# A 31-tap depthwise convolution: from taps on two engines to column-tiled products over shifted copies

## The chip, the cores and the metric

One core of one Trainium2 chip. The metric is the device time of one execution of the whole program in microseconds (us): 3539.51, the median of 3 runs.

## The reference, cut to what matters

Two blocks of two layers each. Block 1 has 768 tokens in its first layer (512 and a context of 256) and carries 512 on from the second. A layer's mixer has three branches; the third is a gated unit followed by a depthwise convolution along the tokens, with 31 taps for each of 256 channels. The other branches: `chunk_gmlp` (gated token mixing) and differential attention.

```python
def dwconv(x, w, b):
    k = w.shape[0]
    y = lax.conv_general_dilated(
        x, w[:, None, :].astype(x.dtype), window_strides=(1,), padding=[(k // 2, k // 2)],
        dimension_numbers=("NWC", "WIO", "NWC"), feature_group_count=x.shape[-1])
    return y + b

def conformer_conv(pc, P):
    a, g = jnp.split(pc, 2, axis=-1)
    y = dwconv(a * jax.nn.sigmoid(g), P["conv_w"], P["conv_b"])
    return jax.nn.silu(layer_norm(y, P["ln_c_g"], P["ln_c_b"]))

def chunk_gmlp(pa, P):
    z = jax.nn.gelu(pa)
    u, v = jnp.split(z, 2, axis=-1)
    v = layer_norm(v, P["ln_v_g"], P["ln_v_b"])
    b, n, _ = v.shape
    vb = v.reshape(b, n // CHUNK, CHUNK, A_HEADS, A_HEAD_DIM)
    gate = jnp.einsum("hpq,bnqhd->bnphd", P["w_s"], vb) + P["b_s"].T[:, :, None]
    return u * gate.reshape(b, n, A_WIDTH)

    # of a block, for each layer:
    pa, q, k, v, pc = project(h, P, rope)
```

The two segments (512 tokens and 256) are convolved each for itself.

## The kernel before

**Products.** A product of precision fp32 is made of three matmuls (L639) over pairs of a rounded part `h` and a rest `l`. Weights stream from HBM in pieces `wr` (two buffers, L274, issued by the sync queue, SP); ScalarE rounds a piece to `wh` (L286), VectorE subtracts to get `wl` (L287); there are three buffers of each. `need` asks for a piece and has the next ones loaded and split (two splits and four loads ahead).

**A layer of block 1** (`b1_layer`). The products of the convolution branch come first (`c`), their results go through the gate (`glu`, L984 on ScalarE, L985 on VectorE; in layer 0 the first half of the channels also through L1059 and L1060) into `cy`: channels on partitions, two tiles of 128 channels, a segment of 512 tokens and in layer 0 one of 256, with 15 zeros at each end. Then follow the products `at` (gated token mixing, six banks of 128 tokens in layer 0, four in layer 1; eight pieces of the contraction), `kt` (keys, six banks in both layers), `qt` (queries) and `vt` (values). A pool of six PSUM banks serves them in turn.

**What lies between `at` and `kt`.** ScalarE takes the gelu of each bank into `z` (L1143). VectorE normalises half of it: statistics (L1145, L1146), the inverse root (L405 to L414), three steps for each `z` (L1153 to L1155). Then TensorE multiplies by the gate's weights (`gt`, L1158: four matmuls of 64 columns), VectorE applies the gate (L1161), TensorE transposes (`yaT`, L1164). The order of TensorE's instructions has these among the matmuls of `kt`.

**Side work.** Each `need` calls `aside`: one or two steps of the modulation vectors (`gv`, L357: a step is four column-tiled fp32 matmuls with 32 columns of weights and 512 moving columns; the trace shows two records for each matmul), whose inputs `g` are loaded by SP (L316, two buffers), and four taps of the convolution.

**Taps.** `ca` gathers the result. The first channel tile is VectorE's: a tap is one instruction for each segment (L1114). The second is GpSimd's: a multiplication into a part of `Q` (L1117), an addition (L1118). Tap 0 is ScalarE's (L1112). `conv(31)` after `kt` asks for what is left.

**What sets the order.** A list scheduler puts each engine's instructions, SP's transfers among them, in one order; each engine runs them in it, and an instruction waits at its place for what it needs.

Of the kernel before, what the change touches and what calls it, by code (L numbers as in the profile page):

```python
# [20 lines left out]
P = 128  # L21
# [107 lines left out]
def _conv(w):  # L129
    """[taps, C] -> [128, C/128 * taps]"""  # L130
# [15 lines left out]
def make_cols():  # L146
    """Per-channel vectors, channels on partitions."""
# [35 lines left out]
def make_mix_cols(l):  # L183
    """What the mixer of a layer of block 1 needs on chip besides its weights."""
    return _layout([
        ("cw", 62, lambda I: _conv(I["conv_w"][l])),
# [12 lines left out]

def bias_table(rpb):  # L200
    """[8, 15, 31] -> [8, 128 (row of the pair, query column), 14 * 64 (row offset, key column)], masked
    outside the window."""
# [16 lines left out]
# ---------------------------------------------------------------- the program  # L219
class Kern:  # L220
    def __init__(self, ctx, tc, ap):
# [20 lines left out]
        # weight stream  # L242
# [7 lines left out]
        # the weights of an output product wait until the attention before it is under way  # L250
# [3 lines left out]
        self.kept = {}  # pools of weights that stay for both parts of the tokens  # L254
# [14 lines left out]
    # -- weights: loaded and split ahead of their use  # L269
# [42 lines left out]
    # -- conditioning vectors  # L312
# [73 lines left out]
    def gemv_until(self, layer, n=1):  # L386
        """At most the vectors of the layers before this one."""
# [9 lines left out]
    # -- small pieces  # L397
# [665 lines left out]
    def b1_layer(self, l, norm):  # L1063
# [11 lines left out]
        with ExitStack() as kvc:  # L1075
# [5 lines left out]
            with ExitStack() as c:  # L1081
# [38 lines left out]
                for t in range(31):  # L1120
                    tap(1, t)
# [694 lines left out]
```

## Time and profile before

| | us |
|---|---|
| median of 3 runs (3536.82 to 3546.21) | 3539.51 |
| span of the profiled execution | 3542.8 |
| TensorE busy in it | 3361.6 |
| VectorE busy | 2431.3 |
| ScalarE busy | 1384.4 |
| GpSimd busy | 353.8 |

The page has no time for the profiled execution other than its span, which lies within the range of the runs. Busy time is a sum over the whole span; the windows and the timeline show single stages. A row of a timeline gives the start, the duration, the engine, the line and the operation, what is written and read, and the idle time before it with what ended it. Matmuls are pipelined: the distance of their starts, not their duration, tells what each costs. `b1l0` is layer 0 of block 1, `b1l1` layer 1.

### The profile page before, as it was taken

How to read it: one execution, taken by the hardware profiler on the slowest of the kernel's cores; microseconds unless marked ns; L12 is line 12 of the kernel's file. 1: busy time of each engine (PE TensorE's matmuls, PEld its weight loads, DVE VectorE, ACT ScalarE, POOL GpSimd, SP SyncE). 2: the span in 40 equal slices, each digit the busy share in tenths (PEclk: the TensorE clock that was granted, in tenths of full speed). 3: DMA queues.
4: the chain of work that ended last, by engine and by line, in shares of the span. 5: the costliest groups of instructions: out<-in, count | busy, mean ns of one | idle time of the engine just before them, and what ended most of it. 6: DMA issues, size and time to landing. Idle time of an engine off the chain costs nothing.

```text
span 3542.8 us, 49269 instructions
## 1 busy us (share of the span) xinstructions
PE 3361.6 (95%) x19440; PEld 2803.6 (79%) x19440; DVE 2431.3 (69%) x4171; ACT 1384.4 (39%) x2548; POOL 353.8 (10%) x310
## 2 busy tenths in 40 slices
PE   8589899999996889999999999999999999999998
PEld 5366788888885679877887778888888878898887
DVE  6967857565559786888653887667564777765445
ACT  4115742222233265222423775312222556653233
POOL 1930000000007210000101111000000100010001
PEclk9899999999998899999999999999999999999999
DMA  6233214333321113555422013344332220032332
GB/s 235 84 101 95 87 48 143 109 122 107 110 90 52 55 43 119 171 180 179 139 82 66 24 35 102 96 125 129 120 104 66 84 61 19 13 114 89 96 95 72
DMA packets 106775, 341.72 MB, mean 96 GB/s; under 512 B 12528, under 2 KB 15600, under 8 KB 106544
## 3 DMA queue, kind: packets, MB, share of 16 engines
q1 hardware_dynamic: 106544, 338.57, 30.9%
q8 instruction: 153, 2.51, 0.3%
q14 instruction: 78, 0.64, 0.1%
HBM read 318.27 MB, written 9.44 MB: 93 GB/s over the span
## 4 chain that ended last, share of the span: by engine, by line
PE 83%; DVE 8%; ACT 2%; issue 1%; DMA 1%; ACTq 0%; POOLq 0%; POOL 0%; DVEq 0%
PE b1l0o L639 2%; PE b2l0o L639 1%; PE b2l1o L639 1%; PE b2l0y L639 1%; PE b1l0y L639 1%; PE b1l1o L639 1%; DVE b1l1ca L1114 1%; PE b1l0qt L639 1%; PE b2l0qat L639 1%; PE b2l1qp L639 1%; PE b2l0vbt L639 1%; PE b1l0vt L639 1%; DVE wl L287 1%; PE gv L367 1%; PE b1l0kt L639 1%
## 5 line engine op out<-in xcount | busy, mean ns | idle before, releaser
L286 ACT CAST wh<-wr 128x1024 fp32r<-128x1024 f32 (+2 forms) x368 | 355.6, 967 | 877.2 <-issue 86.3
L287 DVE TENSOR_TENSOR wl<-wr,wh 128x1024 fp32r<-128x1024 f32 (+2 forms) x368 | 422.1, 1148 | 354.5 <-ACT wh L286 351.6
L341 DVE SCALAR_TENSOR_TENSOR ga<-g,cv,ga 128x1024 f32<-128x1024 f32 x252 | 310.0, 1279 | 4.5 <-DMA g<-in_wmod_dram 4.1
L1114 DVE SCALAR_TENSOR_TENSOR b1l0ca<-b1l0cy,b1l0half,b1l0ca 128x512 f32<-128x512 f32 (+1 forms) x60 | 74.8, 1298 | 0.0
L1118 POOL TENSOR_TENSOR b1l0ca<-b1l0Q,b1l0ca 128x512 f32<-128x512 f32 (+1 forms) x60 | 74.1, 1255 | 0.2
L1117 POOL TENSOR_TENSOR b1l0Q<-b1l0cy,b1l0half 128x512 f32<-128x512 f32 (+1 forms) x60 | 62.4, 1059 | 73.6 <-DVE b1l0cy L985 73.6
L357 PE MATMUL gv<-g,sil 128*32 128x512 f32 x128 | 32.2, 658 | 29.0 <-DMA g<-in_wmod_dram 28.9
L1087 POOL MEMSET b1l1cy<- 128x30 f32 x1 | 0.1, 127 | 584.2 <-PE b1l0y L639 584.2
L493 POOL TENSOR_TENSOR b2l0nas<-b2l0rx,b2l0rx 128x512 f32<-128x512 f32 (+1 forms) x2 | 3.4, 1686 | 535.6 <-DVE b2l0rx L813 535.6
L1403 POOL TENSOR_SCALAR b1l1rx<-b1l1rx 128x768 f32<-128x768 f32 x8 | 17.1, 2135 | 382.0 <-ACT b2l0t0c L581 371.7
L1118 POOL TENSOR_TENSOR b1l1ca<-b1l1Q,b1l1ca 128x512 f32<-128x512 f32 x30 | 47.5, 1584 | 1.2
L1114 DVE SCALAR_TENSOR_TENSOR b1l1ca<-b1l1cy,b1l1half,b1l1ca 128x512 f32<-128x512 f32 x30 | 44.2, 1472 | 1.1 <-issue 0.6
L1117 POOL TENSOR_TENSOR b1l1Q<-b1l1cy,b1l1half 128x512 f32<-128x512 f32 x30 | 42.0, 1418 | 29.1 <-issue 29.1
L1158 PE MATMUL b1l1gt<-b1l1z,b1l1mc 128*128 128x64 f32 x32 | 5.9, 348 | 40.3 <-DVE b1l1z L1155 36.6
L1158 PEld LDWEIGHTS b1l1gt<-b1l1z,b1l1mc 128*128 128x128 f32 x32 | 5.7, 260 | 41.4 <-DVE b1l1z L1155 37.0
L493 POOL TENSOR_TENSOR b2l1a2s<-b2l1rx,b2l1rx 128x256 f32<-128x256 f32 x2 | 2.3, 1161 | 347.4 <-DVE b2l1rx L1378 347.4
L357 PEld LDWEIGHTS gv<-g,sil 128*32 128x32 f32 x128 | 4.4, 112 | 40.9 <-DMA g<-in_wmod_dram 34.3
L493 POOL TENSOR_TENSOR b2l1nas<-b2l1rx,b2l1rx 128x256 f32<-128x256 f32 x2 | 1.5, 742 | 344.3 <-DVE b2l1rx L813 344.3
L850 POOL TENSOR_TENSOR b2l0q<-b2l0QA,b2l0q 64x768 fp32r<-64x768 f32 x6 | 11.3, 1884 | 184.9 <-DVE b2l0VB L682 151.1
L370 ACT COPY gs<-gv 128x512 f32<-128x512 f32 x24 | 14.1, 587 | 36.5 <-PE gv L357 28.7
L858 POOL TENSOR_TENSOR b1l0K<-b1l0KT,b1l0K 64x768 fp32r<-64x768 f32 x6 | 10.9, 1817 | 148.7 <-ACT b1l0K L857 148.5
L343 DVE TENSOR_SCALAR ga<-g,cv 128x1024 f32<-128x1024 f32 x36 | 25.5, 747 | 0.0
(11665 smaller groups left out, 12138.7 us busy)
## 6 DMA issues: line engine op xcount, KB each, us to landing
wr<-in_wts_dram SPq DMA_DIRECT2D x288, 512.0 KB, 3.6
g<-in_wmod_dram SPq DMA_DIRECT2D x176, 512.0 KB, 4.0
wr<-in_wts_dram SPq DMA_DIRECT2D x64, 384.0 KB, 3.1
wr<-in_wts_dram SPq DMA_DIRECT2D x64, 320.0 KB, 2.9
b1l0KT<-in_wmod_dram SPq DMA_DIRECT2D x6, 512.0 KB, 7.0
b1l0Q<-in_wmod_dram SPq DMA_DIRECT2D x6, 512.0 KB, 8.6
inx<-in_x_dram SPq DMA_DIRECT2D x8, 384.0 KB, 8.9
b1l0K<-b1l0K SPq DMA_DIRECT2D x16, 192.0 KB, 2.8
```

What stands on the lines that cost most here:

```text
L286: self.nc.scalar.copy(hi, raw)
L287: self.nc.vector.tensor_tensor(out=lo, in0=raw, in1=hi.bitcast(F32), op=SUB)
L341: nc.vector.scalar_tensor_tensor(out=self.gacc[c], in0=g, scalar=v, in1=self.gacc[c], op0=MUL, op1=ADD)
L343: nc.vector.tensor_scalar(out=self.gacc[c], in0=g, scalar1=v, scalar2=None, op0=MUL)
L357: nc.tensor.matmul(self.gacc[32 * e:32 * e + 32, :], self.sil[:, 2 * k + j, :], g[:, h * 512:h * 512 + 512], start=k == 0, stop=k == 3, ti ...
L367: nc.tensor.matmul(self.gacc[32 * e:32 * e + 32, :], self.ones[:, 0:32], acc[c][:, h * 512:h * 512 + 512], tile_position=(0, 32 * e))
L370: nc.scalar.copy(s, self.gacc)
L639: self.last_mm = self.nc.tensor.matmul(o, s, m[:, sl], start=start and j == 0, stop=stop and j == 2)
L1114: nc.vector.scalar_tensor_tensor(out=dst, in0=src, scalar=s, in1=dst, op0=MUL, op1=ADD)
L1117: nc.gpsimd.tensor_tensor(out=m, in0=src, in1=s.to_broadcast([P, w]), op=MUL)
L1118: nc.gpsimd.tensor_tensor(out=dst, in0=m, in1=dst, op=ADD)
L1403: nc.gpsimd.tensor_scalar(out=X[d], in0=X[d], scalar1=ALPHA, scalar2=None, op0=MUL)
```

## The change

The convolution becomes products. Four shifted copies of the gated input lie under one another on the partitions: group `4 i + k` of `XS` holds, in its partitions 32 j to 32 j + 31, channels 32 k to 32 k + 31 of channel tile `i`, shifted by `j` tokens. A matmul whose stationary operand `cw` (128 x 32: for each of the four shifts a diagonal of 32 tap weights) meets such a group does four taps for 32 channels; eight of them, each four tokens further on, do all 31 (the 32nd weight is zero). The four `k` write to the four quarters of the columns (`tile_position=(0, 32 * k)`) of one bank. ScalarE then halves the result, adds the bias and writes `ca`.

The copies are transfers from SBUF to SBUF on SP: 64 in layer 0 (32 partitions of 540 values, or of 284 for the segment of 256 tokens), 32 in layer 1. `XS` lies in one tile `U` with `KT` and `Q`, which come to be written after it is read. `cw` comes as an input of its own (`convw`, 1 MB for each layer) by a transfer of its own. `Q` no longer lends its place to GpSimd's products, nor to the last two `z`. The products stand between those of `kt` and of `qt`. The taps, and their place in `aside`, are gone. The rest of the diff takes comments out.

```diff
+C_TAPS = 31
-        ("cw", 62, lambda I: _conv(I["conv_w"][l])),
...
+def conv_blocks(w):
+    out = np.zeros((4, 32, 2, 8, 4, 32), np.float32)
+    c = np.arange(32)
+    for t in range(C_TAPS):
+        out[t % 4, c, :, t // 4, :, c] = w[t].reshape(2, 4, 32).transpose(2, 0, 1)
+    return out.reshape(P, 2048)
...
-            KT = kv.tile([P, 4, T], F32, name=b + "KT")
-            Q = kv.tile([P, nq, 512], F32, name=b + "Q")
+            span = sum(w + 28 for _, w in segs)
+            U = kv.tile([P, max(8 * span, 4 * T + nq * 512)], F32, name=b + "U")
+            XS = U[:, :8 * span].rearrange("p (g w) -> p g w", w=span)
+            KT = U[:, :4 * T].rearrange("p (h t) -> p h t", t=T)
+            Q = U[:, 4 * T:4 * T + nq * 512].rearrange("p (t d) -> p t d", d=512)
             Kr = kv.tile([P, 6, 512], F32, tag="KV", name=b + "Kr")
-            cy = [kv.tile([P, 2, w + 30], F32, name=b + f"cy{r}") for r, (_, w) in enumerate(segs)]
+            cy = [kv.tile([P, 2, w + 31], F32, name=b + f"cy{r}") for r, (_, w) in enumerate(segs)]
...
-                half = self.sm.tile([P, 62], F32, tag="half", name=b + "half", bufs=1)
-                nc.vector.tensor_scalar(out=half, in0=self.mcol("cw"), scalar1=0.5, scalar2=None, op0=MUL)
-                ca = [self.xp.tile([P, T], F32, tag="x", name=f"{b}ca{i}") for i in range(2)]
+                cw = c.enter_context(tc.tile_pool(name=b + "cw", bufs=1, reuse_waits="tile")).tile([P, 2, 8, 4, 32], F32, name=b + "cw")
+                nc.sync.dma_start(out=cw, in_=self.ap["convw"][l].rearrange("p (i g k c) -> p i g k c", i=2, g=8, k=4))
+                offs = [sum(w + 28 for _, w in segs[:r]) for r in range(len(segs))]
+                for i in range(2):
+                    for r, (_, w) in enumerate(segs):
+                        for k in range(4):
+                            for j in range(4):
+                                nc.sync.dma_start(out=XS[32 * j:32 * j + 32, 4 * i + k, offs[r]:offs[r] + w + 28],
+                                                  in_=cy[r][32 * k:32 * k + 32, i, j:j + w + 28])
+                ca = []
+
+                def conv():
+                    for i in range(2):
+                        ca.append(self.xp.tile([P, T], F32, tag="x", name=f"{b}ca{i}"))
+                        for r, (x0, w) in enumerate(segs):
+                            ps = pp.tile([P, w], F32, tag="mm", name=f"{b}cv{i}{r}")
+                            for g in range(8):
+                                for k in range(4):
+                                    nc.tensor.matmul(ps[32 * k:32 * k + 32, :], cw[:, i, g, k], XS[:, 4 * i + k, offs[r] + 4 * g:offs[r] + 4 * g + w],
+                                                     start=g == 0, stop=g == 7, tile_position=(0, 32 * k))
+                            nc.scalar.activation(out=ca[i][:, x0:x0 + w], in_=ps, func=AF.Identity, scale=0.5, bias=self.mcol("cb", i, 1))
+
                 tmp = c.enter_context(tc.tile_pool(name=b + "pt", bufs=2, reuse_waits="tile"))
-                def tap(i, t):
...
-                for t in range(31):
-                    tap(1, t)
...
-                    conv(4)
...
-                    z = (self.xp.tile([P, T], F32, tag="x", name=f"{b}z{i}") if i < 4 else
-                         Q[:, i])
+                    z = self.xp.tile([P, T], F32, tag="x", name=f"{b}z{i}")
...
-                conv(31)
+                conv()
                 ps = self.tproj(pp, b + "q", H, no, 512, b + "q")
```

SP in layer 0, around the first weights of `kt`. A number behind a name tells buffers apart. Before, `wr_570` is the last piece of `at`'s weights, `wr_812` the first of `kt`'s:

```order
L274 DMA wr_570<-in_wts_dram 128x1024
L274 DMA wr_812<-in_wts_dram 128x1024
L316 DMA g_831<-in_wmod_dram 128x1024
L316 DMA g_833<-in_wmod_dram 128x1024
L316 DMA g_889<-in_wmod_dram 128x1024
L274 DMA wr_883<-in_wts_dram 128x1024
```

The same place after; `wr_569` is the last piece of `at`'s weights, `wr_754` the first of `kt`'s:

```order
L1124 DMA b1l0U<-b1l0cy_137 32x540 x4
L284 DMA wr_569<-in_wts_dram 128x1024
L1124 DMA b1l0U<-b1l0cy_137 32x540 x14
L1124 DMA b1l0U<-b1l0cy_138 32x284 x16
L1124 DMA b1l0U<-b1l0cy_137 32x540 x14
L1124 DMA b1l0U<-b1l0cy_138 32x284 x16
L284 DMA wr_754<-in_wts_dram 128x1024
L326 DMA g_765<-in_wmod_dram 128x1024
```

The two pieces of weights stood next to one another; now 60 copies stand between them. In layer 1 two copies come ahead of the third piece of `at`'s weights, ten ahead of the fourth, and twenty between that and the first of `kt`'s.

VectorE in layer 0, before, where it splits the second piece of `kt`'s weights (`wr_883`) and comes to the statistics of `z`:

```order
L1114 SCALAR_TENSOR_TENSOR b1l0ca_675<-b1l0cy_139,b1l0half,b1l0ca_675 128x256
L382 TENSOR_TENSOR mod_2_1008<-gt_1003,cols 128x8
L287 TENSOR_TENSOR wl_996<-wr_883,wh_995 128x1024
...
L1114 SCALAR_TENSOR_TENSOR b1l0ca_675<-b1l0cy_138,b1l0half,b1l0ca_675 128x512
L1145 BN_STATS b1l0bst_1062<-b1l0z_1060 128x6
```

After, the end of the steps on `z` and the split of the first piece of `kt`'s weights (`wr_754`):

```order
L1166 TENSOR_TENSOR b1l0z_980<-b1l0z_980,b1l0mc 128x256
L1166 TENSOR_TENSOR b1l0z_985<-b1l0z_985,b1l0mc 128x256
...
L1166 TENSOR_TENSOR b1l0z_995<-b1l0z_995,b1l0mc 128x256
L297 TENSOR_TENSOR wl_864<-wr_754,wh_863 128x1024
```

Two pieces of `kt`'s weights were split ahead of the statistics; now the first is split behind all steps on `z`.

TensorE after, layer 0, from the end of `kt` to the first matmuls of `qt`:

```order
L649 MATMUL b1l0kt_1140<-wh_1200,inHl_121 128x512
L649 MATMUL b1l0kt_1140<-wh_1200,inHh_120 128x512
L649 MATMUL b1l0kt_1140<-wl_1201,inHh_120 128x512
L1136 MATMUL b1l0cv_1461<-b1l0U,b1l0cw 32x512 x32
L1136 MATMUL b1l0cv_1495<-b1l0U,b1l0cw 32x256 x32
L1136 MATMUL b1l0cv_1530<-b1l0U,b1l0cw 32x512 x32
L1136 MATMUL b1l0cv_1564<-b1l0U,b1l0cw 32x256 x32
L367 MATMUL gv_1610<-g_1260,sil 32x512 x2
L367 MATMUL gv_1610<-g_1262,sil 32x512 x2
L649 MATMUL b1l0qt_1598<-wh_1250,inHl_107 128x512
L649 MATMUL b1l0qt_1598<-wh_1250,inHh_106 128x512
```

The convolution's 128 matmuls stand in one piece, with no other product among them.

## Rows read from the trace of the kernel before

**Rows 1.** The page, parts 1 and 4: busy us (share); shares of the chain

```profile
PE 3361.6 (95%) x19440; PEld 2803.6 (79%) x19440; DVE 2431.3 (69%) x4171; ACT 1384.4 (39%) x2548; POOL 353.8 (10%) x310
...
PE 83%; DVE 8%; ACT 2%; issue 1%; DMA 1%; ACTq 0%; POOLq 0%; POOL 0%; DVEq 0%
```

**Rows 2.** Windows: length; busy (instructions) of each engine; PEclk, DMA share, GB/s

```profile
170.00:180.00 10.00, 0.00 (x0) 0.00 (x0) 9.96 (x12) 0.00 (x0) 10.00 (x11) 0.51 0.00 1
228.00:320.00 92.00, 91.47 (x420) 63.26 (x412) 65.80 (x188) 27.28 (x41) 0.00 (x0) 1.00 0.42 135
1107.00:1195.00 88.00, 45.96 (x187) 36.15 (x186) 71.94 (x81) 9.42 (x17) 70.07 (x50) 0.73 0.12 36
```

**Rows 3.** The page, part 5: busy us, mean ns | idle before

```profile
L1114 DVE SCALAR_TENSOR_TENSOR b1l0ca<-b1l0cy,b1l0half,b1l0ca 128x512 f32<-128x512 f32 (+1 forms) x60 | 74.8, 1298 | 0.0
...
L357 PEld LDWEIGHTS gv<-g,sil 128*32 128x32 f32 x128 | 4.4, 112 | 40.9 <-DMA g<-in_wmod_dram 34.3
```

**Rows 4.** Timeline of TensorE in the two layers: start, duration, what, [idle before]

```profile
71.91 0.39 PE L639 MATMUL b1l0at<-wh,inHl 128*128 128x512 f32 x1
...
146.33 1.92 PE L357 MATMUL gv<-g,sil 128*32 128x512 f32 x4 [20.35 <-DMA g<-in_wmod_dram]
...
184.14 1.94 PE L1158 MATMUL b1l0gt<-b1l0z,b1l0mc 128*128 128x64 f32 x8 [16.65 <-issue]
...
227.64 1.06 PE L357 MATMUL gv<-g,sil 128*32 128x512 f32 x8
...
1084.71 0.39 PE L639 MATMUL b1l1at<-wh,b1l0Hl 128*128 128x512 f32 x1
...
1162.61 1.97 PE L1158 MATMUL b1l1gt<-b1l1z,b1l1mc 128*128 128x64 f32 x8 [36.57 <-DVE b1l1z L1155]
...
1194.81 0.40 PE L639 MATMUL b1l1qt<-wh,b1l0Hl 128*128 128x512 f32 x1
```

**Rows 5.** Chain of waits, 60 to 330 us: start, us, engine, what, records

```profile
208.21 0.84 PE b1l0gt L1158 x8
...
220.01 7.70 PE b1l0kt L639 x33
...
227.71 0.99 PE gv L357 x8
```

**Rows 6.** Timeline of TensorE, two modulation steps back to back

```profile
34.47 1.48 PE L357 MATMUL gv<-b1l0KT,sil 128*32 128x512 f32 x10
...
35.79 0.60 PE L357 MATMUL gv<-b1l0Q,sil 128*32 128x512 f32 x2
```

**Rows 7.** All transfers of line 1675, its own view: count, min/median/max ns

```profile
L1675 SPq DMA_DIRECT2D b2l1kh<-b2l1kh x3: 573/584/591, 2861.0 to 2865.4; - x3
...
DMA to landing us min/median/max: 2.1/2.6/3.8
```

**Rows 8.** Timeline of SP, copies of 64 partitions

```profile
322.73 8.02 SPq L860 DMA_DIRECT2D b1l0K<-b1l0K  x8
```

**Rows 9.** The page, part 6: issues, KB each, us to landing

```profile
wr<-in_wts_dram SPq DMA_DIRECT2D x288, 512.0 KB, 3.6
```

**Rows 10.** Timeline of VectorE: gated input of layer 0, of layer 1

```profile
74.75 2.97 DVE L1060 SCALAR_TENSOR_TENSOR b1l0cy<-b1l0cy,b1l0cbs,b1l0KT 128x512 f32<-128x512 f32 x2
...
1087.72 0.68 DVE L985 SCALAR_TENSOR_TENSOR b1l1cy<-b1l1cy,b1l1c10L 128x512 f32<-128x512 f32 x1
```

**Rows 11.** Timeline of ScalarE after `at` of layer 0

```profile
119.38 1.30 ACT L1143 ACTIVATE b1l0Q<-b1l0at 128x512 f32<-128x512 f32 x2
...
120.58 1.04 ACT L286 CAST wh<-wr 128x1024 fp32r<-128x1024 f32 x1
```

**Rows 12.** VectorE by line, 228 to 300 us: busy us, mean ns

```profile
L287 DVE TENSOR_TENSOR wl<-wr,wh 128x1024 fp32r<-128x1024 f32 x6 | 7.3, 1224 | 1.3 <-ACT wh L286 1.3
...
L947 DVE TENSOR_TENSOR b1l0kns<-b1l0Kr,b1l0kS 128x256 f32<-128x256 f32 x8 | 3.0, 419 | 0.0
...
L413 DVE SCALAR_TENSOR_TENSOR b1l0knr2q<-b1l0knr2q,b1l0knr2h 128x16 f32<-128x16 f32 x3 | 0.5, 177 | 0.1
```

More of the change, by code (lines that the diff above doesn't have):

```diff
@@ L1087, in b1_layer @@
                     nc.gpsimd.memset(cy[r][:, :, 0:15], 0.0)
-                    nc.gpsimd.memset(cy[r][:, :, w + 15:w + 30], 0.0)
+                    nc.gpsimd.memset(cy[r][:, :, w + 15:w + 31], 0.0)
                 if last:
@@ L1102, in b1_layer @@
                     nc.sync.dma_start(out=self.mcols, in_=self.ap["mcols"][l])
-                half = self.sm.tile([P, 62], F32, tag="half", name=b + "half", bufs=1)
-                nc.vector.tensor_scalar(out=half, in0=self.mcol("cw"), scalar1=0.5, scalar2=None, op0=MUL)
-                ca = [self.xp.tile([P, T], F32, tag="x", name=f"{b}ca{i}") for i in range(2)]
-                tmp = c.enter_context(tc.tile_pool(name=b + "pt", bufs=2, reuse_waits="tile"))
-                def tap(i, t):
-                    for r, (x0, w) in enumerate(segs):
-                        src, dst, s = cy[r][:, i, t:t + w], ca[i][:, x0:x0 + w], half[:, 31 * i + t:31 * i + t + 1]
-                        if t == 0:
-                            nc.scalar.activation(out=dst, in_=src, func=AF.Identity, scale=s, bias=self.mcol("cb", i, 1))
-                        elif i == 0:
-                            nc.vector.scalar_tensor_tensor(out=dst, in0=src, scalar=s, in1=dst, op0=MUL, op1=ADD)
-                        else:
-                            m = Q[:, t % 2 * 2 + r, :w]
-                            nc.gpsimd.tensor_tensor(out=m, in0=src, in1=s.to_broadcast([P, w]), op=MUL)
-                            nc.gpsimd.tensor_tensor(out=dst, in0=m, in1=dst, op=ADD)
@@ L1120, in b1_layer @@
-                for t in range(31):
-                    tap(1, t)
-                taps = [(0, t) for t in range(31)]
-                def conv(n):
-                    for a in taps[:n]:
-                        tap(*a)
-                    del taps[:n]
+                cw = c.enter_context(tc.tile_pool(name=b + "cw", bufs=1, reuse_waits="tile")).tile([P, 2, 8, 4, 32], F32, name=b + "cw")
+                nc.sync.dma_start(out=cw, in_=self.ap["convw"][l].rearrange("p (i g k c) -> p i g k c", i=2, g=8, k=4))
@@ L1799, in host_arrays @@
         "mcols": np.stack([np.concatenate([f(I) for _, _, f in make_mix_cols(l)[0].values()], axis=1) for l in range(2)]),
+        "convw": np.stack([conv_blocks(I["conv_w"][l]) for l in range(2)]),
         "bias": c(bias_table(I["l0_rpb_2"])),
```

## The prediction

> **What bounds the kernel now.** I read the page first. TensorE is busy for 95% of the span, and the chain of work that ended last is TensorE for 83% and VectorE for 8% [rows 1]. So time is won only where TensorE stands still, and the windows say where that is. From 228 to 320 us it is busy for 91.47 of 92.00 us: work saved elsewhere doesn't help there, and what is won ahead of it is kept. In the key product of layer 1 (1107 to 1195) it is busy for 45.96 of 88 us, while VectorE is busy for 71.94 and GpSimd for 70.07. In the 10 us from 170 both of these are busy throughout, TensorE does nothing, and its granted clock is 0.51, its 1.2 GHz level [rows 2]. What they do there is the taps: 60 on VectorE in layer 0 at 1298 ns [rows 3], on GpSimd two instructions for each tap.
>
> The timeline of TensorE shows what these holes wait for [rows 4]. Layer 0, from the first `at` at 71.91 to the modulation step at 227.64, takes 155.7 us. It has a hole of 20.35 us that ends with a transfer of `g`, and one of 16.65 us before the gate's first product. Neither is a slow transfer: on VectorE the split of the weights and the normalisation of `z` stand among taps, the sync queue waits for the split, and `g` waits in that queue. In layer 1, from 1084.71 to 1194.81 (110.1 us), the hole is 36.57 us, ended by VectorE's last step on `z`.
>
> **Part 1: the taps go.** VectorE and GpSimd lose all of them. What TensorE then has between the same two points, at full clock, is: 144 matmuls of `at` and 144 of `kt` at 7.70/33 = 0.233 us, 67.2 us; eight modulation steps at 0.99, 7.9; six gate products at 0.84, 5.0 [rows 5]; some 2.3 for transposes, an estimate. Layer 0: 82.4 us. In layer 1, 96 and 144 matmuls give 56.0, four gates 3.4, transposes 0.9: 60.3 us.
>
> **Part 2: the convolution becomes TensorE's work.** Layer 0 gets 64 matmuls of 512 columns and 64 of 256, in groups of four, one for each quarter of the columns; layer 1 gets 64 of 512. They stand between `kt` and `qt`, where nothing covers them: they count in full. The nearest thing in the trace is the modulation step, four column tiles of 32 with fp32 operands and 512 columns. Two such steps, 16 records in four passes, begin at 34.47 and their last records at 35.79: (35.79 - 34.47)/3 = 0.44 a pass, two passes to a group, 0.88 us [rows 6]. So layer 0 pays 16 x 0.88 + 16 x 0.44 = 21.1 us and layer 1 14.1 us. A step by itself took 0.99 [rows 5]; by that price the two layers would pay 4 us more, the upper bound. Evacuation is four reads by ScalarE in layer 0 and two in layer 1 (six banks are there, `qt` needs those of `kt` first): nothing.
>
> Each weight load of such a step took 0.112 us [rows 3], and passes 0.44 apart leave no room for two of them to each matmul [rows 6]. The Trainium skill (TensorE: Matmul & The Clock Gate, Part 3: Packing small matmuls) says that a weight load overlaps running matmuls only where the row group differs, and here all four share it. By that rule the loads would be exposed; the trace doesn't agree, with passes 0.44 apart. What it would cost is a rival below.
>
> **Part 3: the copies.** 64 transfers of 32 partitions in layer 0 and 32 in layer 1 enter the sync queue. They are ordered behind the gated input, and ahead of the first weights of `kt`, of the `g` behind these, and of all that follows. No transfer of before is just that. The nearest is the copy of 32 partitions from SBUF to SBUF, at a median 584 ns of issue and 2.6 us to land [rows 7]. I take 0.6 us each, since with that spacing five are under way at a time. The bound above is the row of eight copies of 64 partitions, 8.02/8 = 1.0 us [rows 8]; below, half of 0.6 if issue is shorter for half the bytes.
>
> Layer 0: the first part of the gated input is ready at 74.75 + 2.97/2 = 76.2 [rows 10]. Then 64 x 0.6 = 38.4, and 0.6 for a load of `at` between them: `kt`'s weights are issued at 115.2, land 3.6 us later [rows 9], are rounded in 1.04 [rows 11] and subtracted in 1.22 [rows 12]: ready at 121.0. `at` ends at 71.91 + 33.6 + 1.0 for a modulation step + 0.4 for the tail of the product before it = 106.9. A **new wait of 14.1 us**. VectorE alone would give nearly the same: the order puts that subtract behind the whole `z` chain, which is 106.9 + 0.65 for a gelu + 0.6 for statistics (estimate) + 11 x 0.177 for the root + 18 x 0.42 + 1.22 = 118.9 [rows 11, 12]. So a faster queue wins 2 us at most.
>
> Layer 1: the second half of the copies follows the gated input at 1087.72 + 0.68 = 1088.4 [rows 10]; 20 x 0.6 later the weights are issued, at 1100.4, and could be ready at 1106.3. There the subtract stands behind the root and three steps of `z`: `at` ends at 1107.1, and 0.65 + 0.6 + 1.9 + 3 x 0.42 + 1.22 = 5.7 gives 1112.8. A wait of 5.7 us.
>
> I add 6 us in layer 0 and 4 in layer 1 for what else can be late: matmuls at half clock after the new wait, the splits of `at`'s last weights, and `g`. This is a choice, between 0 and twice as much.
>
> **Sum.** Layer 0: 82.4 + 21.1 + 14.1 + 6 = 123.6 against 155.7, 32.1 won. Layer 1: 60.3 + 14.1 + 5.7 + 4 = 84.1 against 110.1, 26.0 won. Together 58.1. The span of the profile, 3542.8, lies within the runs and 3.3 above their median, so I take the gain from the median: 3539.5 - 58.1 = **3481 us**. The matrix loads with the copies (1 MB more for each layer) are issued tens of us ahead and are costed at nothing; if the first held up `at`, it would be by the landing of one load, some 4 us.
>
> **Rivals.**
>
> *Less late than I allow.* The 10 us of allowances are not needed and the queue is quick: 12 us less, 3469. For it: after 228 the same engines keep TensorE at 99%. Against it: every hole of before left matmuls at half clock behind it.
>
> *The queue takes 1.0 us for a copy.* Then layer 0 loses 64 x 0.4 = 25.6, layer 1 (1088.4 + 20 + 5.9 = 1114.3 against 1112.8) 1.5: 3508. For it, the row of 64 partitions [rows 8]; against it, that those move twice the partitions.
>
> *Weight loads exposed.* Eight loads of 0.112 for each of 48 groups, 43 us: 3524. Against it speak the 0.44 us between passes [rows 3, 6].
>
> *Slower: the queue becomes the bound.* The copies come at p us each, and all weights of `kt` stand behind them. The gain is 58.1 - 64 (p - 0.6) - 20 (p - 0.93), nothing at p = 1.37. If a copy had to land before the next one, at the least landing of 2.1 us [rows 7], it would be 58.1 - 96 - 23.4 = -61: 3601. For it: no stretch of before has 64 copies in a row. Against it: these rows start copies 0.6 apart with landings of 2.6. The Trainium skill (DMA: Bandwidth & Descriptors, Rules for kernel authors) says that under 64 KB a transfer is mostly overhead, with about 2 us of fixed cost; the copies have 69 and 36 KB, and taken in turn they would cost what this rival says. The rows agree with the 2 us as a landing time, not as a spacing.
>
> *Slower too: column tiles of the convolution don't run side by side.* Three times the price is added, 3 x (21.1 + 14.1) = 106: 3587. Only [rows 6] speaks against it, but plainly.
>
> **How the numbers follow.** Forecast 3481, by itself 3468 to 3497 with the allowances and bounds above: 63%. Less late 10%; queue at 1.0 us 17%; loads exposed 4%; queue as bound 4%; tiles in turn 2%. About 0.3% (10.6 us) is what a measurement of this kernel can tell from no change, so the edge is at 3529: faster 0.90, same 0.04 (the upper ends of the second and third rivals), slower 0.06. The range of 8 in 10 leaves out the last three rivals and the upper part of the second: 3461 to 3515.
>
> **What would show it.** In the profile after: no taps and no holes of 20, 17 and 37 us; one wait before `kt` of about 14 us (layer 0) and 6 (layer 1), ended by VectorE's split of the weights; the convolution's groups 0.88 us apart, 21 and 14 us in all; copies 0.6 apart. Wrong: copies 1 us or more apart, a wait before `qt` for copies, passes of 0.87, or waits for `g` in the later part of `kt`.

## The result, and the profile after

The changed kernel takes **3493.56 us** (median of 4 runs, 3491.70 to 3496.89), the kernel before 3540.56 in the same session (4 runs, 3536.82 to 3546.21): a ratio of 0.9862 with a 95% interval of 0.9848 to 0.9876, 47 us or 1.4% faster. The forecast was 3481, its range 3461 to 3515. The profiled executions differ by more than the medians do, 3542.8 against 3490.3 us, since the one of before lies 2 us above its median and the one of after 3 us below.

Parts 1 and 4 of the page of after, which answer to [rows 1]. TensorE has 384 records more (192 matmuls, two records each) and 27 us more of work, GpSimd 222 us less; TensorE's share of the chain that ended last is 91% instead of 83%.

```profile
PE 3388.5 (97%) x19824; PEld 2814.2 (81%) x19824; DVE 2263.5 (65%) x4079; ACT 1383.5 (40%) x2548; POOL 131.5 (4%) x130
...
PE 91%; DVE 5%; ACT 2%; DMA 1%; issue 1%; SPq 0%; ACTq 0%; POOLq 0%; POOL 0%; DVEq 0%
```

Windows of both layers, from the first `at` to the end of the modulation step behind `kt`, or to the first `qt` (length; busy of PE, PEld, DVE, ACT, POOL; PEclk, DMA share, GB/s), of before:

```profile
71.91:228.64 156.73, 104.16 (x431) 67.02 (x430) 137.65 (x169) 25.46 (x41) 134.40 (x120) 0.83 0.26 85
1084.71:1194.81 110.10, 68.06 (x282) 53.85 (x281) 92.13 (x96) 20.05 (x31) 88.38 (x60) 0.78 0.14 43
```

and of after:

```profile
74.65:207.47 132.82, 118.77 (x688) 72.25 (x686) 55.55 (x167) 28.41 (x45) 0.00 (x0) 0.95 0.41 129
1063.21:1146.14 82.93, 78.10 (x409) 54.83 (x408) 38.57 (x105) 21.60 (x34) 0.00 (x0) 0.96 0.29 83
```

Layer 0 is 23.9 us shorter, layer 1 27.2. Of the other 1.4 us of the difference of the two spans, `at` begins 2.7 us later (74.65 against 71.91) and the rest behind layer 1 takes 3.8 us less. No run ties either to the change: three of the kernels below have the order of after up to that point, on every engine, and begin `at` at 71.97, 72.45 and 74.85. For the 3.8 us no run shows a cause.

The timeline of TensorE, which answers to [rows 4] (start, duration, what, idle before): one wait ahead of layer 0's `kt`, two short ones in layer 1, and the convolutions where the step behind `kt` and the first `qt` wait for them.

```profile
123.88 0.79 PE L649 MATMUL b1l0kt<-wh,inHl 128*128 128x512 f32 x1 [14.04 <-ACT wh L296]
...
185.83 20.85 PE L1136 MATMUL b1l0cv<-b1l0U,b1l0cw 128*32 128x512 f32 x256
206.50 1.04 PE L367 MATMUL gv<-g,sil 128*32 128x512 f32 x8
...
1087.39 0.51 PE L649 MATMUL b1l1kt<-wh,b1l0Hl 128*128 128x512 f32 x1 [1.62 <-ACT wh L296]
...
1091.57 0.80 PE L649 MATMUL b1l1kt<-wl,b1l0Hh 128*128 128x512 f32 x1 [3.21 <-DVE wl L297]
...
1132.27 13.94 PE L1136 MATMUL b1l1cv<-b1l1U,b1l1cw 128*32 128x512 f32 x128
1146.14 0.51 PE L649 MATMUL b1l1qt<-wh,b1l0Hl 128*128 128x512 f32 x1
```

The timelines of the sync queue, ScalarE and VectorE around that wait. 60 copies follow each other in 39.23 us, 0.654 us each; the first weights of `kt` are issued behind them, at 119.01; ScalarE waits 12.25 us for that transfer and rounds it, and `kt` begins. VectorE has been done with `z` since 119.5 and waits too.

```profile
76.25 2.75 SPq L1124 DMA_DIRECT2D b1l0U<-b1l0cy  x4
...
79.68 39.23 SPq L1124 DMA_DIRECT2D b1l0U<-b1l0cy  x60
119.01 0.53 SPq L284 DMA_DIRECT2D wr<-in_wts_dram  x1
```

```profile
122.79 1.04 ACT L296 CAST wh<-wr 128x1024 fp32r<-128x1024 f32 x1 [12.25 <-DMA wr<-in_wts_dram]
```

```profile
118.77 0.75 DVE L1166 TENSOR_TENSOR b1l0z<-b1l0z,b1l0mc 128x256 f32<-128x256 f32 x2
123.86 1.23 DVE L297 TENSOR_TENSOR wl<-wr,wh 128x1024 fp32r<-128x1024 f32 x1 [4.35 <-ACT wh L296]
```

### The profile page after: what moved, and what is told of

Same layout as the page of the kernel before. It is cut to its first block, busy times and chain, and to the rows that moved or that the text cites. A ratio compares the mean times of both kernels' runs of the same rounds, so it can differ in the third digit from the quotient of the medians.

```text
span 3490.3 us, 49902 instructions
## 1 busy us (share of the span) xinstructions
PE 3388.5 (97%) x19824; PEld 2814.2 (81%) x19824; DVE 2263.5 (65%) x4079; ACT 1383.5 (40%) x2548; POOL 131.5 (4%) x130
## 4 chain that ended last, share of the span: by engine, by line
PE 91%; DVE 5%; ACT 2%; DMA 1%; issue 1%; SPq 0%; ACTq 0%; POOLq 0%; POOL 0%; DVEq 0%
PE b1l0o L649 2%; PE b2l0o L649 1%; PE b2l1o L649 1%; PE b1l1o L649 1%; PE b2l0y L649 1%; PE b1l0y L649 1%; PE b1l0kt L649 1%; PE b1l1kt L649 1%; PE gv L367 1%; PE b1l0qt L649 1%; PE b1l0at L649 1%; PE b1l1vt L649 1%; PE b1l0vt L649 1%; PE b2l0qat L649 1%; PE b2l1qp L649 1%; PE b2l0vbt L649 1%
## 5 line engine op out<-in xcount | busy, mean ns | idle before, releaser
L649 PE MATMUL b1l0kt<-wh,inHl 128*128 128x512 f32 x48 | 20.0, 416 | 14.0 <-ACT wh L296 14.0
L380 ACT COPY gs<-gv 128x512 f32<-128x512 f32 x24 | 14.1, 586 | 39.4 <-PE gv L367 32.4
L353 DVE TENSOR_SCALAR ga<-g,cv 128x1024 f32<-128x1024 f32 x36 | 25.5, 746 | 0.0
L1714 DVE TENSOR_TENSOR b2l1kl<-b2l1kp,b2l1kh 64x512 fp32r<-64x512 f32 (+1 forms) x32 | 17.7, 554 | 10.9 <-ACT b2l1kh L1713 10.0
L649 PE MATMUL b1l1kt<-wl,b1l0Hh 128*128 128x512 f32 x48 | 20.3, 422 | 3.2 <-DVE wl L297 3.2
L1713 ACT CAST b2l1kh<-b2l1kp 64x512 fp32r<-64x512 f32 (+1 forms) x32 | 15.2, 475 | 18.1 <-PE b2l1kp L649 11.9
L649 PE MATMUL b1l1kt<-wh,b1l0Hl 128*128 128x512 f32 x48 | 19.8, 413 | 1.6 <-ACT wh L296 1.6
L377 PE MATMUL gv<-ga,ones 128*32 128x512 f32 x144 | 21.0, 605 | 0.0
L1136 PE MATMUL b1l0cv<-b1l0U,b1l0cw 128*32 128x512 f32 (+1 forms) x256 | 20.8, 486 | 0.0
L649 PE MATMUL b1l0vt<-wh,inHl 128*128 128x512 f32 x48 | 20.8, 433 | 0.0
L649 PE MATMUL b1l1kt<-wh,b1l0Hh 128*128 128x512 f32 x48 | 20.5, 426 | 0.0
L649 PE MATMUL b1l0vt<-wl,inHh 128*128 128x512 f32 x48 | 20.5, 426 | 0.0
```

Source lines behind the costliest of these rows:

```text
L353: nc.vector.tensor_scalar(out=self.gacc[c], in0=g, scalar1=v, scalar2=None, op0=MUL)
L377: nc.tensor.matmul(self.gacc[32 * e:32 * e + 32, :], self.ones[:, 0:32], acc[c][:, h * 512:h * 512 + 512], tile_position=(0, 32 * e))
L380: nc.scalar.copy(s, self.gacc)
L649: self.last_mm = self.nc.tensor.matmul(o, s, m[:, sl], start=start and j == 0, stop=stop and j == 2)
L1136: nc.tensor.matmul(ps[32 * k:32 * k + 32, :], cw[:, i, g, k], XS[:, 4 * i + k, offs[r] + 4 * g:offs[r] + 4 * g + w], start=g == 0, stop=g ...
L1713: nc.scalar.copy(hi[0:64, c0:c1], kp[r])
```

## The experiments

Three questions stood open: whether the prices of convolution and copies are those of the forecast, what took the 8 us that layer 0 lacks of it, and whether the holes of before came from where the prediction put them. Stage lengths below are the two windows above, 132.8 and 82.9 us for after, 156.7 and 110.1 for before. The kernel before had medians of 3543.9 to 3545.3 in these sessions, 3 to 5 us above that of the session of after, so a difference from after is no surer than that; stage lengths are what the readings rest on.

### The price of the convolution

Two of its eight groups of four taps stay (`conv_short`):

```diff
-                            for g in range(8):
+                            for g in (0, 7):
```

> The changed kernel with two of the eight steps of each convolution group (it leaves out the other six, so 24 of the 32 tap positions are missing). Theory: the convolution lies on the path in full, 20.7 us in layer 0 and 13.9 in layer 1 as traced, so a quarter of it should stay, 5.2 and 3.5, and the program should end 26 us earlier, near 3468 (against 3493.6). Rival: something else ends last beside it (evacuations, the next weights, g), and the time stays within 6 us of 3493.6.

Measured: 3468.09 us. Timeline of TensorE:

```profile
183.16 5.37 PE L1136 MATMUL b1l0cv<-b1l0U,b1l0cw 128*32 128x512 f32 x64
...
1113.29 3.64 PE L1136 MATMUL b1l1cv<-b1l1U,b1l1cw 128*32 128x512 f32 x32
```

A quarter of the work takes a quarter of the time in both layers, and the kernel gains what they lose, 25.5 us: nothing covers the convolution, and a group of 512 columns costs 0.87 us (13.87/16 in layer 1 of after). In this run `at` begins at 71.97.

### The price of the copies

Each copy is issued twice (`copies_twice`):

```diff
-                            for j in range(4):
+                            for j in (0, 1, 2, 3) * 2:
```

> The changed kernel with each shifted copy made twice (128 transfers in layer 0, 64 in layer 1). Theory: the wait of 14.0 us before the key product of layer 0 is the sync queue's, 0.65 us a copy; 64 more make it 14 + 42 = 56 us, and in layer 1 the wait of 4.8 us becomes some 23. The time is some 60 us longer, near 3553. Rival: the queue isn't what the weights wait for, the copies overlap, and the time stays within 10 us of 3493.6.

Measured: 3546.11 us; layer 0 took 174.4 us, layer 1 96.6. Timelines of the sync queue and of TensorE:

```profile
77.48 79.48 SPq L1124 DMA_DIRECT2D b1l0U<-b1l0cy  x121
```

```profile
162.01 0.80 PE L649 MATMUL b1l0kt<-wh,inHl 128*128 128x512 f32 x1 [54.38 <-ACT wh L296]
```

Twice the copies, 0.657 us each: 125 of them instead of 64 stand ahead of the weights, and the wait grows by 40.3 us, what 61 more take at that price (40.1). So the wait in layer 0 grows with the sync queue's issue time and with nothing else. Layer 1 lost 13.7 us and not 18, and not at the weights of `kt`, for which TensorE waits 0.5 us there: in this kernel's order all four gates and their turns stand ahead of `kt` and not among its matmuls, and TensorE waits 11.7 us for the steps between them. This run says nothing of the queue in layer 1.

In the next, a copy takes both channel tiles at once, so that half as many transfers carry the same bytes (`pair_copies`):

```diff
-                for i in range(2):
-                    for r, (_, w) in enumerate(segs):
...
+                for r, (_, w) in enumerate(segs):
...
-                                nc.sync.dma_start(out=XS[32 * j:32 * j + 32, 4 * i + k, offs[r]:offs[r] + w + 28],
-                                                  in_=cy[r][32 * k:32 * k + 32, i, j:j + w + 28])
+                            nc.sync.dma_start(out=XS.rearrange("p (i k) w -> p i k w", i=2)[32 * j:32 * j + 32, :, k, offs[r]:offs[r] + w + 28],
+                                              in_=cy[r][32 * k:32 * k + 32, :, j:j + w + 28])
```

> The changed kernel with both channel tiles in one copy: 32 transfers of twice the size in layer 0, 16 in layer 1, on the sync queue as before. If a copy is paid by the transfer (0.65 us), the 32 of layer 0 take 21 us, the weights are there before VectorE has done its steps on z, and the wait falls from 14.0 to the 9.5 us which VectorE's own order leaves (4.35 us less, what it was idle before the split): near 3488. If it is paid by the partition row or the byte, 32 copies take the same 42 us, and the time is 3493 or, since the first copy waits for both tiles, some us more.

Measured: 3499.08 us, a miss. The sync queue:

```profile
78.54 21.14 SPq L1123 DMA_DIRECT2D b1l0U<-b1l0cy  x31
```

0.68 us a transfer: the price goes by the transfer, not by its bytes. Layer 0 waits 9.0 us as expected, yet takes 129.1, only 3.7 less than after; layer 1 takes 91.4, 8.4 more. The timeline of TensorE shows what that is, from the last matmul of `at` to the first of `kt`:

```profile
1081.11 0.40 PE L649 MATMUL b1l1at<-wl,b1l0Hh 128*128 128x512 f32 x1
1086.94 1.94 PE L1168 MATMUL b1l1gt<-b1l1z,b1l1mc 128*128 128x64 f32 x8 [5.43 <-DVE b1l1z L1165]
...
1099.20 0.78 PE L649 MATMUL b1l1kt<-wh,b1l0Hl 128*128 128x512 f32 x1
```

TensorE doesn't wait for the weights. As in `copies_twice`, the order has changed: three of the four gates, with most of their turns, stand ahead of `kt`, where no matmuls cover VectorE's steps on `z`, and the holes between them (one of 5.43 us and several of 0.4 to 1) lie open; in after the gates stand among the matmuls of `kt`. Why the scheduler moved them is not shown.

### The copies from another queue

GpSimd, which has no taps now, issues them (`pool_copies`):

```diff
-                                nc.sync.dma_start(out=XS[32 * j:32 * j + 32, 4 * i + k, offs[r]:offs[r] + w + 28],
+                                nc.gpsimd.dma_start(out=XS[32 * j:32 * j + 32, 4 * i + k, offs[r]:offs[r] + w + 28],
```

> The changed kernel with the copies issued by GpSimd instead of the sync queue; nothing else is edited, but the order of the split of the weights and of the modulation steps follows. Theory: the weights of the key product come before the end of the product ahead, and the waits of 14.0 us (layer 0) and 4.8 us (layer 1) go. Some of the modulation steps move into the product ahead, where four of them are still in halves. 17 to 20 us less: near 3475. Rival: GpSimd takes over 1.5 us for a copy, so the convolution waits for it (in layer 0 there are some 96 us from the first copy to its start), and the time is 3493 or more.

Measured: 3467.43 us (3465.27 to 3471.29), ratio 0.9784 (0.9767 to 0.9800). Layer 0 takes 118.6 us, layer 1 74.75. Transfers of line 1124, of this kernel and then of after (count, min/median/max ns of one issue), and TensorE in layer 1 of this kernel:

```profile
L1124 POOL DMA_DIRECT2D b1l0U<-b1l0cy x64: 498/498/705, 77.0 to 121.9; - x64
```

```profile
L1124 SPq DMA_DIRECT2D b1l0U<-b1l0cy x64: 507/588/1421, 76.3 to 118.3; - x64
```

```profile
1046.97:1121.72 74.75, 74.75 (x410) 52.54 (x408) 38.72 (x105) 21.80 (x34) 10.07 (x21) 1.00 0.31 91
```

GpSimd is as late with its last copy (121.9 against 118.3) as the sync queue, so it is not that the copies go faster: the weights no longer stand behind them. All waits of layer 1 are gone, and in layer 0 one of 4.5 us for a `g` is left. With the weights in time VectorE has split two pieces of them (at 106.11 and 115.70) before the statistics of `z` begin at 120.82; in after the first is split behind the whole chain.

### The modulation steps

A modulation step is four column tiles, two for each of two `g` tiles; in after, each half runs when its own `g` is there. Here (`whole_steps`) a step waits for both, and its matmuls follow each other:

```diff
-                    for j in range(2):
-                        g = self.graw.pop(j0 + j)
-                        for h in range(2):
+                    gs = [self.graw.pop(j0 + j) for j in range(2)]
+                    for h in range(2):
+                        for j in (1, 0):
```

> The changed kernel with the four matmuls of a modulation step of layer 0 in another order, so that its first one needs the second of its two inputs and the step is not begun before both are there. Theory: what the sum of the prediction missed in layer 0 (23.9 us won between the first gated-mixing matmul and the first query matmul, not 32.1) is modulation steps cut in halves, each half taking 0.98 us as a whole step does; in the order of this kernel five of seven stand whole in the key product, which gives 5 us there and some 3 later: near 3486. The wait of 14 us stays. Rival: halves cost no more than their share, and the shortfall is the clock after the wait: no change, 3493 within 2.

Measured: 3487.41 us (3486.14 to 3490.86), ratio 0.9841 (0.9826 to 0.9856): 6.2 us below after by the medians, though the interval overlaps that of after. Layer 0 is 6.3 us shorter: its steps take 10.8 us instead of 18.7, for one step fewer, which now lies ahead of `at`, and TensorE waits 2.1 us for `g`. Steps on TensorE in after, where x8 is a whole step (as at 206.50 above), x4 a half and x2 the matmul of one column tile, with what stands around them:

```profile
132.25 0.40 PE L649 MATMUL b1l0kt<-wh,inHh 128*128 128x512 f32 x1
132.57 1.05 PE L367 MATMUL gv<-g,sil 128*32 128x512 f32 x4
133.56 0.51 PE L649 MATMUL b1l0kt<-wl,inHh 128*128 128x512 f32 x1
133.90 0.39 PE L649 MATMUL b1l0kt<-wh,inHl 128*128 128x512 f32 x1
...
152.03 1.04 PE L367 MATMUL gv<-g,sil 128*32 128x512 f32 x2
153.01 0.33 PE L1175 MATMUL b1l0yaT<-ident,b1l0z 128*128 128x128 f32 x1
```

From 132.57 to 133.56 is 0.99 us for half a step, what a whole one takes [rows 5], a single tile takes 0.98 (152.03 to 153.01), and the matmuls ahead of the half and behind it take 0.32 and 0.34 us from start to start where others take 0.23. In `kt` of after, six steps lie in 14 such pieces, ten of x4 and four of x2; in this run five of seven there are whole. The last two edits together (`pool_whole`):

> Copies issued by GpSimd and modulation steps kept whole, together. Theory: the two prices are apart from one another, so their gains add, less what the copies' move already mended: in the run with copies on GpSimd the modulation steps of layer 0 took 14.55 us between the first gated-mixing and the first query matmul, in the run with whole steps 10.75 for one step fewer (11.7 with it). 3 us less there and 1 to 3 in the query and value products: 3462 to 3464 against 3467.4. Rival: with whole steps TensorE waits for the second input where it began with the first, as it did for 4.4 us in the run with whole steps, and nothing is left: 3466 to 3469.

Measured: 3468.73 us (3465.40 to 3469.04), ratio 0.9786 (0.9770 to 0.9803): nothing beyond the copies from GpSimd alone. Layer 0 is 2.8 us shorter than with these, with one step fewer in it and with waits for `g` of 6.1 instead of 4.5 us, since a step waits for both of its `g`; and `at` begins 2.7 us later, with that step ahead of it, which takes the rest back.

### Whose taps made the holes

The kernel before, without the taps of one engine. First without VectorE's (`no_vector_taps`; channel tile 0 keeps only its first tap):

```diff
                         elif i == 0:
+                            continue
```

> The kernel before, with VectorE's 30 taps of each segment left out (the first channel tile has tap 0 alone); GpSimd's taps stay. Theory: VectorE's order was the whole delay; what is ahead of TensorE is short even while GpSimd slows VectorE. Layer 0 from the first gated-mixing to the first query matmul falls from 156.7 to some 105 us, layer 1 from 110.1 to some 70: near 3450. Rival: GpSimd's use of the same memory ports is what makes VectorE slow, and the steps on z alone still hold TensorE up: 3490 or more.

Measured: 3518.24 us, 26 below before. Layer 0 takes 156.9 us, as before; layer 1 80.2. TensorE still waits 23.1 us for a `g` and 28.3 for the first gate; in layer 1 the wait for the first gate falls from 36.57 to 11.8 us. Timelines of TensorE and of VectorE in layer 0, with 60 taps gone:

```profile
143.78 1.92 PE L357 MATMUL gv<-g,sil 128*32 128x512 f32 x4 [23.11 <-DMA g<-in_wmod_dram]
...
181.87 1.94 PE L1159 MATMUL b1l0gt<-b1l0z,b1l0mc 128*128 128x64 f32 x8 [28.27 <-issue]
```

```profile
102.19 36.84 DVE L287 TENSOR_TENSOR wl<-wr,wh 128x1024 fp32r<-128x1024 f32 x1 [9.23 <-ACT wh L286]
```

and of GpSimd, the first and last rows that begin within these 36.84 us:

```profile
102.83 1.63 POOL L1118 TENSOR_TENSOR b1l0Q<-b1l0cy,b1l0half 128x256 f32<-128x256 f32 x2
...
137.84 2.66 POOL L1118 TENSOR_TENSOR b1l0Q<-b1l0cy,b1l0half 128x256 f32<-128x256 f32 x2
```

One subtract, 1.22 us in other places [rows 12], takes as long as GpSimd needs for some 40 instructions one after the other. Now without GpSimd's taps, with VectorE's (`no_gpsimd_taps`; channel tile 1 keeps only its first tap); instructions on TensorE, VectorE, ScalarE and the sync queue stand in the same order as before, row for row:

```diff
                         else:
+                            continue
                             m = Q[:, t % 2 * 2 + r, :w]
```

> The kernel before, with GpSimd's 30 taps left out (the second channel tile has tap 0 alone); VectorE's taps stay. Theory: VectorE's taps were slow because GpSimd worked beside them; alone they take some 0.6 instead of 1.30 us in layer 0 and 0.7 instead of 1.47 in layer 1, and the steps on z some 0.4 instead of 1.1. So most of the 52.6 us of idle in layer 0 and of the 42.0 in layer 1 goes even with the taps in the order: 30 us in layer 0, 30 in layer 1, near 3483. Rival: VectorE's order is the delay whatever GpSimd does, and the time stays within 15 us of 3543.

Measured: **3429.28 us**, 115 below before and 64 below after, with all of VectorE's taps, and 54 below what the theory gave. Windows of both layers:

```profile
72.17:163.15 90.98, 90.94 (x431) 62.04 (x429) 65.51 (x169) 25.36 (x41) 0.00 (x0) 1.00 0.43 146
1020.12:1080.91 60.79, 60.79 (x282) 48.70 (x280) 45.06 (x96) 19.77 (x31) 0.00 (x0) 1.00 0.25 78
```

TensorE doesn't stand still for a tenth of a microsecond. VectorE by line in layer 0 (busy us, mean ns | idle before), of before (its taps are in [rows 3]), without VectorE's taps, and without GpSimd's (the two edited kernels have one line more, so L1153 to L1155 of before are L1154 to L1156 there):

```profile
L287 DVE TENSOR_TENSOR wl<-wr,wh 128x1024 fp32r<-128x1024 f32 x9 | 16.0, 1779 | 2.4 <-ACT wh L286 2.4
L1154 DVE TENSOR_TENSOR b1l0z<-b1l0z,b1l0mc 128x256 f32<-128x256 f32 x4 | 4.3, 1109 | 0.0
L1153 DVE TENSOR_SCALAR b1l0z<-b1l0z,b1l0mv,b1l0vrq 128x256 f32<-128x256 f32 x4 | 3.8, 992 | 0.0
L1161 DVE SCALAR_TENSOR_TENSOR b1l0z<-b1l0gt,b1l0mc,b1l0z 128x64 f32<-128x64 f32 x16 | 3.4, 272 | 2.6 <-PE b1l0gt L1158 2.6
```

```profile
L287 DVE TENSOR_TENSOR wl<-wr,wh 128x1024 fp32r<-128x1024 f32 x9 | 51.5, 5718 | 12.6 <-ACT wh L286 12.6
L1156 DVE TENSOR_TENSOR b1l0z<-b1l0z,b1l0mc 128x256 f32<-128x256 f32 x4 | 8.1, 2072 | 0.0
```

```profile
L1114 DVE SCALAR_TENSOR_TENSOR b1l0ca<-b1l0cy,b1l0half,b1l0ca 128x512 f32<-128x512 f32 (+1 forms) x60 | 33.2, 610 | 0.0
L287 DVE TENSOR_TENSOR wl<-wr,wh 128x1024 fp32r<-128x1024 f32 x9 | 11.0, 1221 | 4.9 <-ACT wh L286 4.9
L1156 DVE TENSOR_TENSOR b1l0z<-b1l0z,b1l0mc 128x256 f32<-128x256 f32 x4 | 1.5, 421 | 0.0
L1154 DVE TENSOR_SCALAR b1l0z<-b1l0z,b1l0mv,b1l0vrq 128x256 f32<-128x256 f32 x4 | 1.5, 412 | 0.0
L1162 DVE SCALAR_TENSOR_TENSOR b1l0z<-b1l0gt,b1l0mc,b1l0z 128x64 f32<-128x64 f32 x16 | 3.4, 277 | 6.0 <-PE b1l0gt L1159 6.0
```

The same tap takes 1298 ns beside GpSimd's [rows 3] and 610 without, a subtract 1779 and 1221 on the mean of nine, a step on `z` 1109 and some 421. The step that takes its first input from PSUM (L1161, L1162) takes the same: 272, 275 and 277. No wait of TensorE, VectorE, ScalarE or the sync queue in the two layers of before is put down to GpSimd, so they did not wait for its results or buffers: the instructions themselves were longer. The Trainium skill (SBUF — State Buffer, Who interferes with whom and Summary: rules for kernel authors) says that a VectorE instruction with two inputs in SBUF contends with a GpSimd instruction that reads SBUF, by an exclusive lock, and that the one which comes second blocks until the first has finished. The rows agree for the subtract, the taps and the steps with two inputs in SBUF, and for the one with an input in PSUM. That one of them can last over some forty in a row, 36.84 us, is what the run adds; and the step with one tensor and two columns (L1153, without GpSimd's taps L1154) suffers as well, 992 against 412.

### Versions that keep VectorE's taps

Channel tile 0 goes back to 31 taps on VectorE, and tile 1 alone is column-tiled, with half of the copies; GpSimd computes no taps. These copies come once from GpSimd and once from the sync queue (the diff shows the second):

```diff
+                            nc.sync.dma_start(out=XS[32 * j:32 * j + 32, k, offs[r]:offs[r] + w + 28],
+                                              in_=cy[r][32 * k:32 * k + 32, 1, j:j + w + 28])
...
+                                nc.tensor.matmul(ps[32 * k:32 * k + 32, :], cw[:, 1, g, k], XS[:, k, offs[r] + 4 * g:offs[r] + 4 * g + w],
...
+                            nc.vector.scalar_tensor_tensor(out=dst, in0=src, scalar=s, in1=dst, op0=MUL, op1=ADD)
```

> Channel tile 0 by taps on VectorE as before, channel tile 1 by column-tiled products, its copies (32 in layer 0, 16 in layer 1) issued by GpSimd; GpSimd computes no taps. Theory, from the run without GpSimd's taps (3429, VectorE's 30 taps hidden and TensorE without idle time in both layers): half of the convolution comes on top, 10.3 + 6.9 us: near 3447. Rival: GpSimd's copies slow VectorE as its taps did, or VectorE's order holds up the key product again: 3465 or more.

Measured: 3453.01 us (3448.98 to 3453.99), ratio 0.9741 (0.9725 to 0.9758), 6 us above the theory; in layer 0 a wait of 3.6 us for a `g` is left.

> The same with the copies on the sync queue, where they stand ahead of the first weights of the key product. 32 at 0.65 are 21 us, so these weights are issued near 100 in layer 0, some 9 us before the product ahead ends; what is late then is VectorE's split behind its taps and the steps on z. Theory: 0 to 8 us more than with GpSimd's copies, 3447 to 3455. Rival: the order again puts the split behind all steps on z, as in the run with pairs of copies, a wait of some 9 us in each layer: 3465.

Measured: 3450.64 us (3446.47 to 3455.73), ratio 0.9737 (0.9723 to 0.9752). With 32 copies the queue is no longer late: layer 0 has no wait and takes 105.5 us, against 106.3 with GpSimd's copies, the two ranges overlap, and either queue does.

Last, the kernel before with all 62 taps on VectorE, two channel tiles to each tap, and no convolution on TensorE (`all_vector`):

```diff
                         else:
-                            m = Q[:, t % 2 * 2 + r, :w]
-                            nc.gpsimd.tensor_tensor(out=m, in0=src, in1=s.to_broadcast([P, w]), op=MUL)
-                            nc.gpsimd.tensor_tensor(out=dst, in0=m, in1=dst, op=ADD)
+                            nc.vector.scalar_tensor_tensor(out=dst, in0=src, scalar=s, in1=dst, op0=MUL, op1=ADD)
...
-                    conv(4)
+                    conv(6)
```

> The kernel before with all 62 taps of each layer on VectorE, six at each request for weights and the rest ahead of the norm of the branch; GpSimd has none, TensorE no convolution. Theory: with GpSimd silent a tap is 0.61 us in layer 0 and 0.75 in layer 1, 33 and 22 us more VectorE work than in the run without GpSimd's taps, where VectorE was busy for 93 of 131 us and 45 of 61. Layer 0 just fits, layer 1 lacks some 7 us: 3430 to 3445. Rival: VectorE's order is the bound when it is that full, since splits and steps on z queue behind taps: 3460 or more.

Measured: **3433.59 us** (3430.01 to 3436.67), ratio 0.9688 (0.9674 to 0.9703), 110 us below before in the same session and 60 below after. Its windows:

```profile
72.67:163.87 91.20, 91.17 (x432) 62.02 (x430) 78.99 (x195) 25.45 (x41) 0.00 (x0) 1.00 0.44 146
1021.83:1082.60 60.77, 60.77 (x282) 48.76 (x280) 56.72 (x117) 19.57 (x31) 0.00 (x0) 1.00 0.26 78
```

In these windows VectorE is busy for 79 of 91 and 57 of 61 us, and TensorE waits for nothing. Of the taps 91 of 120 lie in the window of layer 0 and 50 of 60 in that of layer 1; the others come behind it, and the whole costs 4 us more than the run that leaves out half of the convolution.

## Why the prediction was right, and where it was not

**The sum.** Forecast 58 us won in the two stages, measured 51.1 (47 by the medians): 23.9 of 32.1 in layer 0, 27.2 of 26.0 in layer 1. In layer 0, from the first `at` to the step behind the convolution, it is 131.85 us instead of 123.6, and its terms, each from the starts of TensorE's timeline, are:

| layer 0, us | forecast | after |
|---|---|---|
| matmuls of `at` and `kt` | 67.2 | 72.2 |
| eight modulation steps | 7.9 | 17.7 |
| gates, transposes, turns | 7.3 | 7.2 |
| convolution | 21.1 | 20.7 |
| wait ahead of `kt` | 14.1 | 14.0 |
| allowance | 6 | |

Layer 1 took 82.9 us instead of 84.1: matmuls 59.7 against 56.0, where the granted clock was 0.52 from 1091.5 to 1098 us, which the 4 us of allowance paid for; convolution 13.9 against 14.1, waits 4.8 against 5.7, gates and turns 4.5 against 4.3.

**The term that was mis-sized: the modulation steps.** The prediction took a step for 0.99 us, a whole one, eight times. In after six of them lie in 14 pieces that cost as much as wholes, 13.7 us; one is whole, 1.0; and one behind the wait takes 3.0 (124.61 to 127.59), where the granted clock is 0.69 from 124 to 131 us, against 1.00 from 132 on: 17.7 us. Of the 5.0 us over on the matmuls, 16 pieces with 0.2 us more on the two matmuls beside them are 3.2, and those at the lower clock behind the wait about 1; the latter is what the allowance was for, and it was spent on both. In the run with whole steps the steps of the stage fall by 7.9 us, of which one step is 1. The term could have been read before: between the same points the eight steps of the kernel before take 17.6 us as well, four of them whole and four in two pieces each, some at the lower clock. A piece of x4 and the matmul behind it:

```profile
90.21 1.05 PE L357 MATMUL gv<-g,sil 128*32 128x512 f32 x4
91.19 0.51 PE L639 MATMUL b1l0at<-wl,inHh 128*128 128x512 f32 x1
```

I had read the duration of one whole step and not counted the pieces.

**The convolution.** Two bounds were given, 0.88 and 0.99 us a group; the lower one holds, 20.7 and 13.9 us or 0.86 to 0.87 a group, and `conv_short` shows that they count in full. The weight loads are answered too: layer 0 has 256 loads of a median 110 ns, 28 us, within 20.85 us of convolution, so they lie behind the matmuls although all share their rows. The rivals with exposed loads and with tiles in turn are out.

**The copies.** 0.654 us and not 0.6, and still 14.0 us of wait: 64 of them were 3.8 us longer than forecast, but behind them only the rounding stood on the path (`kt` starts with the rounded half, and VectorE's split runs beside it), which is 1 us less, and `at` itself was 2.7 us late. The size was hit partly by luck; the mechanism, the weights' issue behind the copies, is what `copies_twice` shows. Neither rival on the queue came: copies don't wait for each other's landing, and not for 1.0 us.

**A faster queue.** "Wins 2 us at most", since VectorE's order would be as late. That step was wrong: GpSimd's queue won 14.2 us in layer 0, and 26 in all. The order on VectorE is not fixed, as the prediction took it to be: where the weights come in time, their split stands ahead of the chain on `z`.

**The cause of the holes.** The prediction laid them to the splits standing among VectorE's taps and took the taps' 1298 ns as their price. The size of the gain was near all the same, since the change takes away both engines' taps; but it did not name the cause that weighs more: GpSimd's taps made VectorE's instructions longer, a tap 2.1 times, a step on `z` 2.6 times and a subtract 1.5 times on the mean. Without GpSimd's, with VectorE's taps in the same order, all holes of [rows 4] are gone; without VectorE's, with GpSimd's, those of layer 0 are still there, and that of layer 1 is down to 11.8 us, so there VectorE's taps weigh too. Taking away GpSimd's taps alone is worth 115 us (110 where VectorE does them); the change does that and gives 64 back. In the two windows these are 41.8 + 22.1: the convolution 20.7 + 13.9, the waits 14.0 + 4.8, and 7.1 + 3.4 that are left, in layer 0 mostly the halved steps. Had this been read before, by comparing one operation's time inside and outside the stage ([rows 12]: the split 1224, in the stage 1779), the question would have been why TensorE should do the taps at all.

What stays open: why the scheduler put the gates of layer 1 ahead of `kt` in `copies_twice` and `pair_copies`, and why `at` begins at 71.97 to 74.85 us in kernels with one and the same order up to it. With whole steps it begins later still (77.53 and 77.94), with one step more ahead of it.

## What to carry to other kernels

Where VectorE and GpSimd work side by side on SBUF, compare the time of one VectorE operation inside that stage and outside of it before moving work: if it is longer inside, first try the stage with GpSimd silent, even if VectorE then does everything. Work that moves onto the engine that bounds the kernel is paid in full, and its helpers (here 96 copies) are paid by the transfer on the queue that they share with the weights: give them another queue. Count pieces, not operations: half a column-tiled step costs a whole one, and so does a quarter.

## What was not expected of the hardware

- One 128x1024 subtract on VectorE took 36.84 us instead of 1.22, while GpSimd ran some 40 instructions on SBUF back to back; with both engines busy a tap took 1298 ns instead of 610.
- Not only instructions with two tensors in SBUF suffer: the step with one tensor and two columns (L1153) took 992 ns beside GpSimd's taps and 412 without; the statistics of `z` took 400 and 409.
- Small copies from SBUF to SBUF follow each other on the sync queue 0.65 to 0.68 us apart, whether one carries one channel tile or two. GpSimd's issue of one takes 0.498 us against 0.588 at the median, but with its waits its 64 take 44.9 us, no less than the sync queue's.
- Two column tiles, and even one, take as long as four: 0.98 to 0.99 us for 512 columns.
